# Splitting streamed weights one transfer at a time instead of one tile at a time

## The chip, the core and the metric

The kernel runs on one core of a Trainium2 chip. The metric is the device time of one execution in microseconds (us). The core has a matrix engine (TensorE, PE in the profile, its weight loads PEld), a vector engine (VectorE, DVE), a scalar engine (ScalarE, ACT), GpSimd (POOL) and SyncE (SP), which issues the DMA transfers here.

## The reference, cut to what matters

The reference is a stack of six layers on 256 tokens of width 2048, in float32: an RWKV7 mixer, a dilated attention, a pooling mixer, an RWKV7 mixer again, a layer of attention beside an RG-LRU, and an mLSTM layer, with a final norm. Every layer has the form below; the projections with their large weights are most of the work.

```python
for i in range(DEPTH):
    h = _rms_norm(x, norm_w[i])
...
    x = x + y
...
r, k, v, g = [(h + xx * mu[j]) @ w_in[j] for j in range(4)]   # RWKV7, layers 0 and 3
...
return y @ w_out, v_first
```

## The kernel before

Every projection is token-major: `proj` (L238) computes 256 tokens by 512 output columns at a time, in two PSUM tiles `qps`, and runs over the 2048 rows of the weight matrix. Activations stand, and weights are streamed from HBM. To reach float32 accuracy each operand is the sum of a high half (rounded to fp32r) and a low half (the rest), and a product is three matmuls: high activation with high weight, high with low, low with high (L258 to L261).

`weights` (L222) brings one transfer of 512 KB, that is two tiles of 128 rows by 512 columns, into a raw buffer `wr` (pool of 3) by a DMA on the SP queue (L224). Each of the two tiles is then split: ScalarE copies it into a high tile `wh` (L219), and VectorE subtracts that from the raw tile into a low tile `wl` (L220). `wh` and `wl` come from pools of 5 tiles each. In most of the RWKV7 layers every third transfer has its low tiles made on GpSimd instead (`lo_share` = 3). A tile then feeds six matmuls: two token halves by three products. One raw buffer serves two tiles, so it comes free when the second subtraction is done, and a `wh` or `wl` tile comes free when the last of its matmuls is done.

The order on each engine is written by a planner when the program is built: it traces the program in order, simulates a time line, and puts instructions that are ready into each engine's queue. Work beside the stream (attention heads, RWKV7 blocks, conversions of activations) is traced by generators that go on as the stream's pieces are traced (`pump`, `spawn`); the RWKV7 blocks are traced at a higher priority. At run time each engine goes through its queue in that order.

In an RWKV7 layer the first projections follow the mixing of `h` with its shifted difference (L496, on VectorE), then come eight blocks of heads with many small instructions, then the output projection, which adds to the residual (L398). The PSUM pool of `qps` has 2 tiles in the RWKV7 layers and 4 elsewhere. The split of whole activations uses the same helper `split` (L218) on wider tiles, for example `dh` and `dl` of 128 x 1024 in the pooling layer.

Of the kernel before, what the change touches and what calls it, by code (L numbers as in the profile page):

```python
# [12 lines left out]
FR = mybir.dt.float32r  # L13
# [14 lines left out]
# feature-major vectors: name -> rows of the source array (row-major, width), per 128-wide tile  # L28
# [45 lines left out]
def make_tables():  # L74
    """masks of the dilated attention and of the mLSTM, tables of the axial rope"""
    p, t = np.arange(128)[:, None], np.arange(128)[None]
    masks = []
    for dil in (1, 4, 16):
        row = []
        for tt, ss in ((0, 0), (1, 0), (1, 1)):  # L80
            d = (p + 128 * tt) - (t + 128 * ss)
            row.append(np.where((d >= 0) & (d <= 128 * dil) & (d % dil == 0), 0.0, -1e30))
        masks.append(np.concatenate(row, 1))
    f = np.where(p <= t, 0.0, 1e30)
    b = np.where(p >= t, 0.0, 1e30)
    odd = np.concatenate([f, 0 * f, 0 * f, b], 1)
    tok = np.arange(256)
    inv = (10000.0 ** (-np.arange(0, 64, 2) / 64)).astype(np.float32)
    ang = np.concatenate([(tok // 64).astype(np.float32)[:, None] * inv, (tok % 64).astype(np.float32)[:, None] * inv], 1)
    ax = np.stack([np.cos(ang.astype(np.float64)), np.sin(ang.astype(np.float64))], 1).reshape(2, 128, 128)  # L90
    ax = ax.transpose(1, 0, 2).reshape(128, 256)
    f32 = lambda z: np.ascontiguousarray(z, np.float32)
    return {"t_mask": f32(np.stack(masks)), "t_odd": f32(odd), "t_axial": f32(ax)}
# [5 lines left out]
# pools of the whole kernel, with their slots  # L99
KEPT = {"wr": 3, "wh": 5, "wl": 5, "ah": 4, "al": 4, "q4": 8, "z": 4, "ssq": 2, "jk": 1, "rs_v": 2, "rstd": 2, "hrstd": 2,  # L100
# [4 lines left out]
class State:  # L105
    """what a layer starts from: chunks of the normed input"""
# [9 lines left out]
class Builder:  # L116
# [20 lines left out]
    @contextmanager  # L137
    def layer(self):
        """scope of the pools that one layer uses"""
        with ExitStack() as st:  # L140
            self.lctx, self.lpools = st, {}
            yield
            self.lctx, self.lpools = None, None

    # ---------------------------------------------------------------- interleaving
    # Work beside the weight stream is traced by generators. They yield the time, in us of the tensor engine, that
    # what they wait for takes; the stream lets the due ones go on after each of its pieces.
# [37 lines left out]
    # ---------------------------------------------------------------- tiles  # L185
# [31 lines left out]
    # ---------------------------------------------------------------- splits  # L217
# [4 lines left out]
    def weights(self, src, shape):  # L222
        raw = self.t("wr", shape, F32, 3)
        self.nc.sync.dma_start(raw, src)  # L224
        self.wcount += 1
        eng = self.nc.gpsimd if self.lo_share and self.wcount % self.lo_share == 0 else None
        hi, lo = [], []
        for k in range(2):
            hi.append(self.t("wh", [128, shape[2]], FR, 5))
            lo.append(self.t("wl", [128, shape[2]], FR, 5))  # L230
            self.split(hi[k], lo[k], raw[:, k], eng)
        return hi, lo
# [4 lines left out]
    # ---------------------------------------------------------------- products  # L237
    def proj(self, w, col0, n, acts, consume, chunks=None, after=None):  # L238
        """token-major out[t, col0:col0+n] = act^T @ w; acts: (hi, lo) tiles [128, 4, 256], filled in by tasks;
        after[c]: generator to start when chunk c is used."""  # L240
        nc = self.nc
        chunks = list(range(len(acts))) if chunks is None else list(chunks)
        pts = [self.p("ps") for _ in range(2)]
        for c in chunks:
            self.drain(lambda: acts[c] is not None)
            ah, al = acts[c]
            for j in range(2):
                r0 = c * 512 + j * 256
                wh, wl = self.weights(w[r0:r0 + 256, col0:col0 + n].rearrange("(k p) n -> p k n", p=128), [128, 2, n])
                for k in range(2):  # L250
                    kk = j * 2 + k
                    st = c == chunks[0] and kk == 0
                    sp = c == chunks[-1] and kk == 3
                    for t in range(2):
                        o = pts[t][:, :n]
                        sl = slice(t * 128, t * 128 + 128)
                        nn = n
                        for u, v, x in ((ah, wh, 0), (ah, wl, 1), (al, wh, 2)):  # L258
                            for c1 in range(0, n, nn):
                                cs = slice(c1, c1 + nn)  # L260
                                nc.tensor.matmul(o[:, cs], u[:, kk, sl], v[k][:, cs], start=st and x == 0 and c1 == 0, stop=sp and x == 2, skip_group_check=True)  # L261
                    if not sp:
                        self.pump(1.29)
            if after and c in after:
                self.spawn(after[c])
        consume(pts)
        self.pump(1.29)

    def to_fm(self, src, nft, consume):
        """src token-major [128, 2, nft*128]; consume(pair index, psum [128, 2, 256]) per two feature tiles."""  # L270
# [11 lines left out]
    def acts_from(self, src, box, c, scale=None):  # L282
        """(hi, lo) chunk box[c] from a token-major [128, 2, 512]; scale(ft): per-feature column."""
# [15 lines left out]
    # ---------------------------------------------------------------- small maths  # L299
    def rsqrt(self, v, n, pre="rq"):  # L300
        """1/sqrt(v) of a small [128, n] tile (v > 0), to float32 accuracy."""
# [35 lines left out]
    def bcast(self, ap1d, tag, n, bufs=2):  # L337
        """a row of DRAM on all partitions"""
# [4 lines left out]
    # ---------------------------------------------------------------- residual, and the start of the next layer  # L343
# [93 lines left out]
    # ---------------------------------------------------------------- RWKV7  # L437
# [31 lines left out]
    def opened(self, st, u, after):  # L469
        """half a chunk of h, and its difference to the step before; its first instruction behind `after`"""  # L470
# [214 lines left out]
    def rwkv_block(self, ia, b):  # L685
        """heads 4b .. 4b+3, features 256b .. 256b+255"""
# [28 lines left out]
        # ---- normalised k, negated (token-major)  # L715
# [11 lines left out]
        # ---- decay  # L727
# [12 lines left out]
        # ---- v, with the residual of the first layer's v  # L740
# [34 lines left out]
        # ---- feature-major operands, [rt|at] / [ks|bs] for even chunks, swapped for odd ones; the other way round  # L775
        # for heads 2 and 3, so that products of 64 rows take turns on the two halves of the tensor engine's rows
# [49 lines left out]
        # ---- bonus  # L826
# [14 lines left out]
        # ---- per-chunk products  # L841
# [16 lines left out]
        # ---- inverse of the unit triangular 16 x 16 blocks by columns  # L858
# [36 lines left out]
        # ---- v above (or below) the place of the solution, and its product with the strictly lower part  # L895
# [20 lines left out]
        # ---- token-major [ks; bs] for the state  # L916
# [10 lines left out]
        # ---- doubled to 32 x 32 and 64 x 64; Y: transpose of X (whose 32 x 32 blocks off the  # L927
        # diagonal are still zero), R: of X M
# [26 lines left out]
        # the last step has one block of 32 x 32 in each of 64 x 64  # L955
# [23 lines left out]
        # ---- chunks in turn  # L979
# [58 lines left out]
        # ---- group norm, bonus  # L1038
# [28 lines left out]
    # ---------------------------------------------------------------- shared by the other layers  # L1067
# [4 lines left out]
    def silu_part(self, pts, hr, dst):  # L1072
        """dst = p (1 + tanh(hr p)); silu(rstd p) = hr dst"""
# [5 lines left out]
    def log1p_exp(self, e, shape, tag):  # L1079
        """log(1 + e) for e in [0, 1], by 2 atanh(e / (2 + e))"""  # L1080
# [23 lines left out]
    def qk_fm(self, e, nh, gain, rope, dst, box, key):  # L1104
        """rms norm over each head, gain, rope, and the transposes into dst [128, nh, 256]"""
# [18 lines left out]
    # ---------------------------------------------------------------- dilated attention  # L1124
# [29 lines left out]
    def dilated(self):  # L1154
# [68 lines left out]
        def combine(O, ml, flags):  # L1223
            # weights over the dilations; ml[:, 0] holds minus the maxima
# [81 lines left out]
    # ---------------------------------------------------------------- pool mixer  # L1306
# [73 lines left out]
    # ---------------------------------------------------------------- attention and RG-LRU  # L1380
    def even(self):
# [25 lines left out]
        # per-feature constants of the LRU  # L1407
# [193 lines left out]
    # ---------------------------------------------------------------- mLSTM  # L1601
    def odd(self):
# [13 lines left out]
        # ---- gates: g = i - b, M = max(0, cummax g), b = cumsum log sigmoid(f), per direction  # L1616
# [72 lines left out]
        def heads(u, v2, qT, kT, vt):  # L1689
# [4 lines left out]
            for a in range(2):  # L1694
# [10 lines left out]
                # blocks: forward s0 (t0 t1), backward s1 (t0 t1), backward s0 t0, forward s1 t1  # L1705
# [15 lines left out]
                for t in range(2):  # L1721
                    for d in range(2):
                        # the column of ones behind v gives the denominator
# [145 lines left out]
```

## Time and profile before

| | |
|---|---|
| median of three executions | 3269.81 us (3268.89 to 3271.18) |
| profiled execution, first to last instruction | 3273.9 us |
| its own time outside that span | not shown |
| PE busy | 3044.3 us, 93% of the span |
| DVE busy | 2383.0 us, 73% |
| ACT busy | 1789.0 us, 55% |
| POOL busy | 704.3 us, 22% |
| moved by DMA | 577.27 MB, mean 176 GB/s |

Busy times are those of one profiled execution. A matmul's end is modelled, and matmuls overlap, so 93% is not the share of time in which the engine does as much as it can. The layers follow one another at about these times: RWKV7 from 0 to 800 us, dilated attention and pooling from 800 to 1620, RWKV7 from 1620 to 2430, attention with RG-LRU to 2700, mLSTM to the end.

### The profile page before, as it was taken

To read this page: it belongs to the slowest core of one execution; us is meant where nothing else is said; L and a number is where in the kernel's file an instruction comes from. 1 tells how busy PE (TensorE), PEld (TensorE's weight loads), DVE (VectorE), ACT (ScalarE), POOL (GpSimd) and SP (SyncE) were. 2 spreads that over 40 slices of the span, in tenths; PEclk is the share of its full clock that TensorE was granted. 3 is DMA by queue.
4 is the path that set the end of the run, shared out by engine and by line. 5 is a ranking of instruction groups with operands and counts; after the bars stand their busy time and mean duration, and the time that the engine had idled before them with its cause. 6 is when DMAs were issued, how large, how long until landed. Compare 5 with 4: busy or idle time off the path is not lost.

```text
span 3273.9 us, 49521 instructions
## 1 busy us (share of the span) xinstructions
PE 3044.3 (93%) x17128; PEld 2460.4 (75%) x17128; DVE 2383.0 (73%) x5326; ACT 1789.0 (55%) x3504; POOL 704.3 (22%) x555
## 2 busy tenths in 40 slices
PE   5889989998999999999978899889989999999998
PEld 4667767776888888888756777667777788888886
DVE  7788978865667666676596888888567776666765
ACT  4566555544555555655555555544456655554554
POOL 4433433430101100020063224433311110000001
PEclk9999989999999999999988999989999999999999
DMA  5655543366565556666656644533575556666665
GB/s 180 204 187 162 169 147 116 128 196 199 176 179 178 170 174 213 200 212 190 209 163 212 198 144 152 170 112 104 192 225 160 159 180 206 181 197 171 187 185 167
DMA packets 327018, 577.27 MB, mean 176 GB/s; under 512 B 33856, under 2 KB 60776, under 8 KB 326768
## 3 DMA queue, kind: packets, MB, share of 16 engines
q1 hardware_dynamic: 326768, 574.12, 56.4%
q8 instruction: 134, 2.20, 0.3%
q14 instruction: 116, 0.95, 0.1%
HBM read 527.88 MB, written 46.15 MB: 175 GB/s over the span
## 4 chain that ended last, share of the span: by engine, by line
PE 60%; DVE 12%; DMA 5%; ACT 3%; issue 2%; POOL 1%; SPq 0%; ACTq 0%; DVEq 0%; POOLq 0%
PE qps L261 53%; DVE wl L220 3%; PE qtp L276 2%; ACT wh L219 1%; DMA wr<-a_w_out 1%; DMA wr<-a_w_in 1%; DVE e L496 1%; DMA lw<-a_a2x 1%; PE qgm L1727 1%; PE qtp L849 0%; DVE Xc L888 0%; DVE Xc L886 0%; DVE al L220 0%; DVE mb L883 0%; DMA v<-st 0%
## 5 line engine op out<-in xcount | busy, mean ns | idle before, releaser
L220 DVE TENSOR_TENSOR wl<-wr,wh 128x512 fp32r<-128x512 f32 x1580 | 1163.7, 746 | 674.1 <-ACT wh L219 660.7
L219 ACT CAST wh<-wr 128x512 fp32r<-128x512 f32 x1728 | 1055.2, 620 | 991.2 <-PE qps L261 494.9
L261 PE MATMUL qps<-wl,ah 128*128 128x512 f32 x3424 | 1387.4, 405 | 40.5 <-DVE wl L220 40.1
L261 PE MATMUL qps<-wh,al 128*128 128x512 f32 x3424 | 1371.1, 401 | 2.0 <-DVE al L220 2.0
L261 PE MATMUL qps<-wh,ah 128*128 128x512 f32 x3424 | 1270.1, 407 | 63.3 <-DVE st L398 14.5
L261 PEld LDWEIGHTS qps<-wh,ah 128*128 128x128 f32 x3424 | 658.6, 193 | 209.8 <-ACT wh L219 20.8
L261 PEld LDWEIGHTS qps<-wl,ah 128*128 128x128 f32 x3424 | 661.9, 193 | 189.2 <-DVE wl L220 55.2
L261 PEld LDWEIGHTS qps<-wh,al 128*128 128x128 f32 x3424 | 660.7, 193 | 142.0 <-DVE al L220 4.4
L220 POOL TENSOR_TENSOR wl<-wr,wh 128x512 fp32r<-128x512 f32 x148 | 201.1, 1366 | 371.0 <-ACT wh L219 326.5
L1114 POOL TENSOR_TENSOR q<-q,gain 128x1024 f32<-128x1024 f32 (+1 forms) x15 | 35.0, 2334 | 432.4 <-ACT sq L1108 432.4
L276 PE MATMUL qtp<-cst,q 128*128 128x128 f32 x388 | 61.1, 287 | 18.4 <-DMA cst<-consts 6.7
L867 ACT COPY Md<-GM 32x128 f32<-32x128 f32 x128 | 54.8, 428 | 39.7 <-DVE GM L852 38.6
L849 PE MATMUL qtp<-q,q 64*128 64x128 f32 x512 | 69.5, 300 | 6.6 <-DVE GM L852 4.7
L496 DVE SCALAR_TENSOR_TENSOR e<-q,vec,q 128x256 f32<-128x256 f32 x96 | 72.4, 801 | 0.0
L276 PEld LDWEIGHTS qtp<-cst,q 128*128 128x128 f32 x388 | 48.2, 146 | 31.2 <-issue 15.6
L883 DVE TENSOR_TENSOR mb<-mb,Xc 128x120 f32<-128x120 f32 (+14 forms) x240 | 70.2, 292 | 0.3
L219 ACT CAST ah<-st 128x512 fp32r<-128x512 f32 x64 | 38.3, 616 | 58.1 <-DMA st<-mix 57.4
L849 PEld LDWEIGHTS qtp<-q,q 64*128 64x128 f32 x512 | 56.2, 197 | 17.7 <-DVE GM L852 6.8
L220 DVE TENSOR_TENSOR al<-st,ah 128x512 fp32r<-128x512 f32 x64 | 51.9, 818 | 19.1 <-ACT ah L219 19.0
L481 POOL TENSOR_TENSOR q<-q 128x510 f32<-128x510 f32 x12 | 15.7, 1307 | 223.1 <-ACT ah L219 219.6
L498 POOL TENSOR_TENSOR e<-e,q 128x512 f32<-128x512 f32 x32 | 55.3, 1747 | 27.8 <-ACT e L494 23.9
L886 DVE TENSOR_TENSOR Xc<-Xc,mb 128x8 f32<-128x8 f32 x240 | 58.8, 245 | 0.8
(404 smaller groups left out, 3421.2 us busy)
## 6 DMA issues: line engine op xcount, KB each, us to landing
wr<-a_w_in SPq DMA_DIRECT2D x256, 512.0 KB
wr<-b_w_in SPq DMA_DIRECT2D x160, 512.0 KB
wr<-odd_w_in SPq DMA_DIRECT2D x128, 512.0 KB
wr<-even_w_in SPq DMA_DIRECT2D x72, 512.0 KB
wr<-a_w_out SPq DMA_DIRECT2D x64, 512.0 KB
wr<-c_w_in SPq DMA_DIRECT2D x64, 512.0 KB
st<-mix SPq DMA_DIRECT2D x64, 256.0 KB
wr<-c_w_out SPq DMA_DIRECT2D x32, 512.0 KB
```

The costliest lines, as they stand in the source:

```text
L219: self.nc.scalar.copy(hi, src)
L220: (eng or self.nc.vector).tensor_tensor(lo, src, hi.bitcast(F32), OP.subtract)
L261: nc.tensor.matmul(o[:, cs], u[:, kk, sl], v[k][:, cs], start=st and x == 0 and c1 == 0, stop=sp and x == 2, skip_group_check=True)
L276: nc.tensor.transpose(q[:, f, t * 128:t * 128 + 128], src[:, t, (fp * 2 + f) * 128:(fp * 2 + f) * 128 + 128], self.ident)
L496: ins = nc.vector.scalar_tensor_tensor(m[:, f], st.xx[c][:, ft], mu, st.h[c][:, ft], OP.mult, OP.add)
L498: ins = nc.gpsimd.tensor_tensor(m, m, st.h[c][:, a * 2:a * 2 + 2], OP.add)
L849: nc.tensor.matmul(qs[hp][:, c], BK[rs, f, c], AR[rs, f, c], start=True, stop=True)
L867: nc.scalar.copy(Md[rs, :, us].rearrange("p c u -> p u c"), GM2[rs, us, (1 - i // 2) ^ f, rs])
L883: nc.vector.tensor_tensor(mb[:, 0:n], mb[:, 0:n], Xc[:, r:r + 1].to_broadcast([128, n, 8]), OP.mult)
L886: nc.vector.tensor_tensor(Xc[:, r + 1], Xc[:, r + 1], mb[:, 0], OP.add)
L1114: nc.gpsimd.tensor_tensor(e3, e3, gain.unsqueeze(1).to_broadcast([128, 2 * nh, 128]), OP.mult)
L1727: nc.tensor.matmul(qn, Dm[:, blk], vt[:, s, a], start=(i == 0), stop=(i == len(tm) - 1))
```

## The change

A transfer's two tiles are split by one copy and one subtraction over 128 x 2 x 512 elements. The pools `wh` and `wl` hold four buffers of such a pair in place of five single tiles, which is eight tiles' room instead of five in each. `proj` receives views of the two tiles of a pair, and its matmuls are as they were. The reserved scratch for dynamic DMA descriptors at the start of SBUF is set to 1024 bytes per partition instead of its default. Comments and docstrings also go, which moves later line numbers by three.

```diff
-KEPT = {"wr": 3, "wh": 5, "wl": 5, "ah": 4, "al": 4, "q4": 8, "z": 4, "ssq": 2, "jk": 1, "rs_v": 2, "rstd": 2, "hrstd": 2,
+KEPT = {"wr": 3, "wh": 4, "wl": 4, "ah": 4, "al": 4, "q4": 8, "z": 4, "ssq": 2, "jk": 1, "rs_v": 2, "rstd": 2, "hrstd": 2,
...
         eng = self.nc.gpsimd if self.lo_share and self.wcount % self.lo_share == 0 else None
-        hi, lo = [], []
-        for k in range(2):
-            hi.append(self.t("wh", [128, shape[2]], FR, 5))
-            lo.append(self.t("wl", [128, shape[2]], FR, 5))
-            self.split(hi[k], lo[k], raw[:, k], eng)
-        return hi, lo
+        hi, lo = self.t("wh", shape, FR, 4), self.t("wl", shape, FR, 4)
+        self.split(hi, lo, raw, eng)
+        return [hi[:, k] for k in range(2)], [lo[:, k] for k in range(2)]
...
-    nc = bacc.Bacc("TRN2", target_bir_lowering=False, num_devices=1)
+    nc = bacc.Bacc("TRN2", target_bir_lowering=False, num_devices=1, dynamic_dma_scratch_size=1024)
```

## Rows read from the trace of the kernel before

**Rows 1.** The page: busy time by engine, and TensorE's granted clock in 40 slices.

```profile
PE 3044.3 (93%) x17128; PEld 2460.4 (75%) x17128; DVE 2383.0 (73%) x5326; ACT 1789.0 (55%) x3504; POOL 704.3 (22%) x555
...
PEclk9999989999999999999988999989999999999999
```

**Rows 2.** Windows by stage: length, busy us (instructions) of PE, PEld, DVE, ACT, POOL, clock, DMA share, GB/s.

```profile
0.00:200.00 200.00, 148.62 (x635) 114.19 (x636) 152.47 (x239) 111.02 (x223) 82.58 (x68) 0.92 0.59 193
200.00:700.00 500.00, 459.17 (x3722) 361.23 (x3720) 415.22 (x1304) 275.96 (x609) 185.63 (x153) 0.95 0.47 150
...
800.00:1620.00 820.00, 818.41 (x3838) 680.79 (x3838) 552.36 (x942) 460.15 (x837) 75.94 (x51) 1.00 0.62 189
1620.00:1850.00 230.00, 190.06 (x881) 151.78 (x880) 178.85 (x305) 130.22 (x257) 87.27 (x64) 0.90 0.60 190
1850.00:2330.00 480.00, 436.99 (x3525) 341.67 (x3524) 396.33 (x1259) 252.29 (x562) 167.92 (x142) 0.93 0.45 142
```

**Rows 3.** The chain that ended last, whole span: shares by line, pieces (start, us, what).

```profile
by line: PE qps L261 52.8%; DVE wl L220 2.9%; issue 2.1%; PE qtp L276 1.6%; ACT wh L219 1.1%; DMA wr<-a_w_out 1.0%; DMA wr<-a_w_in 1.0%; DVE e L496 0.8%; DMA lw<-a_a2x 0.8%; PE qgm L1727 0.6%; PE qtp L849 0.5%; DVE Xc L888 0.5%; DVE Xc L886
...
1388.31 27.25 PE qps L261 x120
...
2366.70 5.29 DMA wr<-a_w_out
```

**Rows 4.** The same chain, from 1625 to 1850 us, then from 1850 to 2330 us.

```profile
by line: DVE e L496 12.2%; DMA wr<-a_w_in 12.0%; DVE wl L220 10.3%; PE qps L261 9.5%; issue 9.0%; DMA mix<-st 4.3%; ACT wh L219 4.1%; DMA v<-st 3.7%; DVE al L220 3.0%; POOL e L498 2.6%; ACT e L494 2.5%; ACT ah L219 2.1%; DVE q L477 2.0%; DM
...
by line: PE qps L261 25.8%; DVE wl L220 6.4%; DMA lw<-a_a2x 5.5%; issue 4.8%; PE qtp L849 2.6%; DVE Xc L886 2.6%; DVE mb L883 2.1%; DMA st<-mix 1.8%; DVE Xc L888 1.8%; DMA vt<-v 1.8%; PE qtp L731 1.8%; DVE e L755 1.7%; ACT wh L219 1.7%; DVE
981 pieces in order of time: start us, us, what
```

**Rows 5.** Lines 219 and 220: duration ns min/median/max, first and last start us.

```profile
L219 ACT CAST wh<-wr x1728: 600/621/671, 13.8 to 3251.8; 128x512 fp32r<-128x512 f32 x192
L219 ACT CAST dh<-q x4: 1048/1051/1054, 1369.7 to 1457.9; 128x1024 fp32r<-128x1024 f32 x4
...
L220 DVE TENSOR_TENSOR wl<-wr,wh x1580: 617/691/2893, 14.6 to 3252.5; 128x512 fp32r<-128x512 f32 x198
L220 POOL TENSOR_TENSOR wl<-wr,wh x148: 1262/1290/2243, 209.4 to 2390.2; 128x512 fp32r<-128x512 f32 x148
L220 DVE TENSOR_TENSOR dl<-q,dh x4: 1225/1225/1227, 1370.7 to 1459.0; 128x1024 fp32r<-128x1024 f32 x4
```

**Rows 6.** Timeline of ACT and DVE: pairs of splits back to back (start, us).

```profile
2372.07 1.14 ACT L219 CAST wh<-wr 128x512 fp32r<-128x512 f32 x2 [1.72 <-DMA wr<-a_w_out]
...
2406.35 1.28 DVE L220 TENSOR_TENSOR wl<-wr,wh 128x512 fp32r<-128x512 f32 x2
```

**Rows 7.** Waits, whole span: who waited for whom, us in total, times, longest.

```profile
ACT wh L219 <- PE qps L261: 494.9, 569, 9.5
...
PEld qps L261 <- DVE wl L220: 55.6, 35, 5.5
PEld qps L261 <- ACT wh L219: 21.0, 9, 4.3
PE qps L261 <- DVE wl L220: 40.1, 25, 5.1
PE qps L261 <- ACT wh L219: 14.2, 6, 3.9
```

**Rows 8.** Waits of weight loads from 0 to 545 us, then from 1620 to 2430 us.

```profile
PEld qps L261 <- DVE wl L220: 28.3, 19, 3.7
...
PEld qps L261 <- DVE wl L220: 18.5, 9, 5.5
```

**Rows 9.** Timeline of PE behind a stall (start, us, [idle before and releaser]).

```profile
2381.10 0.76 PE L261 MATMUL qps<-wh,ah 128*128 128x512 f32 x1 [3.96 <-DVE st L398]
2381.66 0.63 PE L261 MATMUL qps<-wl,ah 128*128 128x512 f32 x1
2382.09 0.63 PE L261 MATMUL qps<-wh,al 128*128 128x512 f32 x1
```

## The prediction, made before the changed kernel ran

> **What bounds the kernel now.** The table by engine [rows 1] says that TensorE is busy for 93% of the span and VectorE for 73%, but these are means over unlike stages, so the windows come next. From 800 to 1620 us TensorE is busy for 818.41 of 820 us at a granted clock of 1.00, with VectorE at 552 and ScalarE at 460 [rows 2]. There the chain of waits runs through unbroken stretches of the stream: 120 matmuls in 27.25 us [rows 3], 0.227 us each. A tile's six matmuls take 1.36 us and a transfer's twelve 2.72. Both splits of a transfer cost less than that on either engine (below), so in such a stage a cheaper split buys nothing. The last layer runs the same way.
>
> The two RWKV7 layers are different. In their openings (0 to 200 us, 1620 to 1850) TensorE is busy for 149 of 200 and 190 of 230 us, its clock is 0.92 and 0.90, and VectorE is busy for 152 and 179 us [rows 2]. In the blocks (200 to 700, 1850 to 2330) VectorE is at 83% and TensorE at 91 to 92%, again below full clock. The chain in the second opening consists of VectorE's mixing (12.2%), weight transfers (12.0%) and low halves (10.3%); in the second layer's blocks TensorE's stream leads it (25.8%), then low halves (6.4%) and many small pieces [rows 4]. If the change matters, it matters in these layers, some 1,600 us of the span.
>
> The last view is the waits. ScalarE waited for TensorE to free a `wh` tile for 494.9 us in 569 waits [rows 7]: most of the time the buffers are full and the splits are ahead. TensorE in turn waited on splits for little: its weight loads 55.6 us for low tiles (35 waits) and 21.0 for high ones (9); its matmuls 40.1 and 14.2, mostly the same stalls seen a second time [rows 7]. Of the 55.6, the first 545 us hold 28.3 and the second RWKV7 layer 18.5 [rows 8].
>
> **The change, part by part.** *Price of a split.* By the rows for lines 219 and 220, two narrow copies take 2 x 0.621 = 1.242 us and one of 128 x 1024 takes 1.051; two narrow subtractions take 2 x 0.691 = 1.382 and a wide one 1.225 [rows 5]. By duration a transfer saves 0.191 us on ScalarE and 0.157 on VectorE; over 1728/2 = 864 copies and 1580/2 = 790 subtractions that is 165 and 124 us of work. Durations overlap, however, when instructions follow each other: two copies take 1.14 us together and two subtractions 1.28 [rows 6], so the second adds 0.52 and 0.59. With the same overlap of 0.10 a wide one adds 0.95 and 1.125, and a transfer saves 0.09 and 0.06. GpSimd's 148 low tiles become 74 pairs; no row has its wide subtraction, which I bound by 2 x 1.290 = 2.58 us and by that times 1.225/1.382, 2.29. GpSimd is hardly used apart from this in those stages, so it gets nothing in the sum.
>
> What counts is the share on the path. The chain has 2.9% of 3273.9 us = 95 us of low tiles and 1.1% = 36 of high ones [rows 3]. Its first piece that the profile gives is at about 540 us, so I let the second layer stand for the missing part: 10.3% and 4.1% of 225 us for the opening, 6.4% and 1.7% of 320 us for the blocks, 44 and 15 us [rows 4]. On 139 and 51 us the saving by durations (11.4% and 15.4%) is 16 + 8 = 24 us; by spacing (0.06 of 1.18, 0.09 of 1.04, so 5% and 9%) it is 7 + 5 = 12. VectorE in these stages is near 80% busy, where instructions mostly queue, so I take 12. Everywhere else the saving is covered by TensorE's 2.72 us per transfer; without that cover it would be worth the 0.15 us per transfer.
>
> *The first tile comes later.* With narrow splits the first tile of a landed transfer is ready after 0.621 + 0.691 = 1.31 us and the second after 0.621 + 2 x 0.691 = 2.00. With wide ones both are ready after 1.051 + 1.225 = 2.28: 0.97 us later for the first, 0.28 for the second [rows 5]. This costs only where TensorE truly waits on a split, at most 35 + 9 = 44 times [rows 7]. Bounds: 0, if deeper buffers cover all of them, and 44 x 0.97 = 43 us, if each is for a first tile. In the openings VectorE works through the halves one after another with mixing between, so the second tile is what holds TensorE back next; I take 35 x 0.28 = 10 us.
>
> *More buffers.* Five tiles hold 5 x 1.36 = 6.8 us of TensorE's work, eight hold 10.9. With three raw buffers the stream can be about seven transfers ahead instead of five. That could remove at most the 55.6 + 21.0 = 77 us of waits [rows 7], and with each the slow matmuls behind it: after a stall of 3.96 us TensorE went on with 0.43 us between matmuls instead of 0.227 [rows 9], the half level of its clock (1.2 GHz instead of 2.4) for a short while. At least it removes nothing. But 47 of 56 us lie in the RWKV7 layers [rows 8], mostly with VectorE's own work late, which more buffers only let it do a little earlier; I take a fifth of the 77, 15 us.
>
> *Longer instructions in the queues.* An urgent small instruction that becomes ready during a subtraction waits half of 1.225 us instead of half of 0.691 on the average, 0.27 more. From 200 to 700 us VectorE is in splits for about a quarter of the time, so a handover costs some 0.07 us more. Of the 981 chain pieces between 1850 and 2330 [rows 4] perhaps a quarter are such handovers: 17 us in a layer, 34 in two. The lower bound is nothing, because the planner knows the durations and arranges the queue by them. I take 8.
>
> *A raw buffer is held longer.* It is free 0.28 us later per turn, against a transfer that took 5.29 us on the chain [rows 3]. The chain's two large groups of weight transfers, 2.0% or 65 us, are about 12 turns, so 3 us at most; the deeper store pays for it, and I take 0. The queue on SP keeps its order of transfers. The smaller scratch touches no instruction that the trace shows: all transfers of the program's data are issued on SP.
>
> Sum: -12 + 10 - 15 + 8 = -9 us. The profiled execution's span would go from 3273.9 to about 3265. It is 4 us above the median of the runs; the time around the span isn't shown, so I carry the difference over: 3269.8 - 9 = 3261 us.
>
> **The rivals.** *A: the saving stays hidden.* The buffers are full most of the time (494.9 us of ScalarE's waits, [rows 7]), two thirds of the span are TensorE's, and the terms above are small and of both signs. The time is 3270 us. Against it: 139 us of low tiles on the chain. That the larger store never fills, because three raw buffers can't feed it, ends here as well.
>
> *B: the deeper store is what counts.* If three more tiles remove nearly all stalls of the matmuls on splits (54 us) and the other terms are as above with no late first tile, the sum is -54 - 12 + 8 = -58: 3212 us. For it speaks that a stall also costs clock; against it, that so few stalls lie in the blocks, where a store could have been filled beforehand.
>
> *C: slower, by the first tile.* In the two openings TensorE waits for what was just split: 19 + 9 = 28 waits [rows 8]. If the buffers are empty there, each is 0.97 us longer, 27 us, and the deeper store gives nothing: 27 - 12 + 8 = +23, so 3293 us. It decides from the point where more than four or five waits are for a first tile and the store removes none (4 x 0.97 against 12 - 8).
> The Trainium skill, Perfetto Trace Analysis, section Optimizing Scalar/DVE Operations, says that larger operations help where the engine is saturated, and that where ScalarE or VectorE are not saturated but cause bubbles elsewhere, breaking instructions up lets work finish sooner. VectorE at 73% overall and 76 to 78% in the openings is not saturated [rows 2], so by that rule the change goes the wrong way there, and the time would be that of C.
>
> **How the numbers follow.** The forecast, a small gain, has 0.37; A 0.27; B 0.10; C 0.26. Three executions lie within 2.3 us; 0.2%, or 6.5 us, is about what a measurement tells from no change. Faster by more is the forecast and B, 0.47; within it A, 0.27; slower C, 0.26. The planner will write every queue anew, and a chain of a thousand pieces may shift by ten or twenty us for that alone. The range goes from 3225 (the saving by durations, 24, and half of the 54 us of matmul stalls, with the 8 against them: -43, or 3227) to 3292 (next to C), and leaves out about two in ten. The forecast's own range is 3240 to 3263.
>
> **What would show it.** The wide copy at about 1.05 us x864 and the wide subtraction at about 1.23 x790 show the prices. From 800 to 1620 us the same work should take the same 820 us. ScalarE's waits for TensorE should be half as many. If the store is right, the weight loads' waits on `wl` fall below 40 us, and the clock in the openings rises above 0.92 and 0.90; if C is, they rise to 80 or more in the same places. I am wrong if the second RWKV7 layer's blocks change by more than 20 us either way without a change in those waits: then the new order of the queues did it. I am wrong as well if the stages that are TensorE's alone get longer, which would mean that a pair's later release starves the stream.

## The result, and the profile after

The changed kernel takes 3302.98 us (median of four executions, 3295.3 to 3304.65) against 3270.35 for the kernel before, a ratio of 1.0095 (95% interval 1.0075 to 1.0114): 31 us slower by the ratio. The forecast was 3261 with a range up to 3292.

The page of the changed kernel, busy time by engine and the granted clock, beside [rows 1]:

```profile
span 3299.6 us, 47015 instructions
PE 3051.0 (92%) x17128; PEld 2473.7 (75%) x17128; DVE 2296.0 (70%) x4536; ACT 1656.2 (50%) x2640; POOL 712.8 (22%) x481
...
PEclk9989999999999999999989989988989999999999
```

VectorE has lost 87 us of work and ScalarE 133, and the kernel is slower. The prices of the splits were as read from [rows 5]; lines 219 and 220 after, with duration in ns (min/median/max) and first and last start:

```profile
L219 ACT CAST wh<-wr x864: 1027/1053/1083, 21.2 to 3273.5; 128x1024 fp32r<-128x1024 f32 x173
...
L220 DVE TENSOR_TENSOR wl<-wr,wh x790: 1149/1225/3406, 22.3 to 3274.6; 128x1024 fp32r<-128x1024 f32 x198
L220 POOL TENSOR_TENSOR wl<-wr,wh x74: 2342/2394/3247, 206.2 to 2400.9; 128x1024 fp32r<-128x1024 f32 x74
```

The store worked as well. Waits of the changed kernel on splits, beside [rows 7]:

```profile
ACT wh L219 <- PE qps L258: 673.7, 439, 6.2
...
PEld qps L258 <- DVE wl L220: 15.4, 12, 4.3
...
PEld qps L258 <- ACT wh L219: 7.2, 3, 6.0
```

Weight loads waited 15.4 us for low tiles instead of 55.6, and 7.2 for high ones instead of 21.0. Where TensorE waited for the stream, it hardly does now. So the loss is elsewhere. The first transfers of the layers' weights mark the stages (durations in ns of the issue, first and last start in us):

```profile
L224 SPq DMA_DIRECT2D wr<-b_w_in x160: 367/368/384, 785.8 to 1280.6; - x160
...
L224 SPq DMA_DIRECT2D wr<-even_w_in x72: 367/368/1899, 2435.1 to 2687.6; - x72
...
L224 SPq DMA_DIRECT2D wr<-odd_w_out x32: 367/368/368, 3179.6 to 3268.7; - x32
```

Before, these began at 775.3, 2414.0 and 3157.9 us. By these marks the first RWKV7 layer has cost 10 us, and the second brings the delay to 21. With a deeper store a transfer can be issued further ahead of its use, so such marks may be early. The last addition to the residual of each layer (L398 before, L395 after) gives the end of the layer: 791.0 and 801.7 us for the first RWKV7 layer, 2429.6 and 2451.0 for the second, 2777.3 and 2802.4 for attention with RG-LRU (which ends at 2777 us and not at 2700), 3258.8 and 3284.4 for the last. The two RWKV7 layers add 11 and 14 us, the layer after the second adds 4, and the last adds nothing. The last step of the RWKV7 blocks (16 blocks; before it ran from 345.9 to 2384.5 us) moves more:

```profile
L1053 POOL TENSOR_TENSOR yt<-yt,vt x16: 1257/1294/2306, 362.9 to 2423.5; 128x512 f32<-128x512 f32 x16
```

The first block ends 17 us later, the last 39, so the layer ends with half of its last block's delay. Windows of the changed kernel, columns as in [rows 2]:

```profile
200.00:700.00 500.00, 454.37 (x3655) 359.80 (x3654) 404.28 (x1231) 257.77 (x504) 166.77 (x117) 0.93 0.46 144
1850.00:2330.00 480.00, 433.63 (x3411) 339.24 (x3410) 389.03 (x1208) 237.09 (x462) 159.81 (x112) 0.90 0.43 137
800.00:1620.00 820.00, 815.92 (x3835) 679.41 (x3834) 521.97 (x692) 418.16 (x574) 85.81 (x51) 1.00 0.63 190
```

From 800 to 1620 us nothing changes for TensorE (3835 matmuls against 3838 at a clock of 1.00). Beside the blocks it starts fewer matmuls in the same time (3411 against 3525 from 1850 to 2330) at a lower clock (0.90 against 0.93, 0.93 against 0.95 in the first layer). About half of the missing matmuls come from the later start of the stretch: from 1865 to 2345 us there are 3472, again at 0.90. What grew there are handovers within the blocks and the conversions of activations; waits of the changed kernel:

```profile
ACT Md L864 <- DVE GM L849: 55.5, 19, 5.6
...
ACT yt L1030 <- PE qgy L1026: 35.3, 22, 4.7
ACT uv L1006 <- PE qgy L1002: 34.2, 17, 10.3
...
DVE al L220 <- ACT ah L219: 48.0, 26, 6.6
```

Before they were 38.6, 26.5, 27.2 and 24.9 us: 117 together, now 173. The growth is not the loss itself: four narrow pairs (below), as fast as the kernel before, have 46.7, 58.0, 28.8 and 40.0 us in the same groups, 174 together.

### The profile page after: what moved, and what is told of

It is laid out like the page before. It is cut to its first block, busy times and chain, and to the rows that moved or that the text cites. A ratio compares the mean times of both kernels' runs of the same rounds, so it can differ in the third digit from the quotient of the medians.

```text
span 3299.6 us, 47015 instructions
## 1 busy us (share of the span) xinstructions
PE 3051.0 (92%) x17128; PEld 2473.7 (75%) x17128; DVE 2296.0 (70%) x4536; ACT 1656.2 (50%) x2640; POOL 712.8 (22%) x481
## 3 DMA queue, kind: packets, MB, share of 16 engines
q1 hardware_dynamic: 326768, 574.12, 56.4%
## 4 chain that ended last, share of the span: by engine, by line
PE 56%; DVE 11%; DMA 7%; issue 3%; ACT 3%; POOL 2%; SPq 0%; ACTq 0%; DVEq 0%; POOLq 0%
PE qps L258 49%; DVE wl L220 3%; PE qtp L273 2%; DMA wr<-a_w_in 1%; DMA wr<-a_w_out 1%; ACT wh L219 1%; DVE e L493 1%; DMA lw<-a_a2x 1%; PE qgm L1724 1%; DMA v<-st 1%; DMA mix<-st 1%; DVE al L220 0%; PE qtp L846 0%; POOL wl L220 0%; DMA st<-mix 0%
## 5 line engine op out<-in xcount | busy, mean ns | idle before, releaser
L220 DVE TENSOR_TENSOR wl<-wr,wh 128x1024 fp32r<-128x1024 f32 x790 | 1027.9, 1304 | 695.2 <-ACT wh L219 693.1
L258 PE MATMUL qps<-wh,ah 128*128 128x512 f32 x3424 | 1378.3, 405 | 58.3 <-ACT st L604 16.6
L258 PE MATMUL qps<-wh,al 128*128 128x512 f32 x3424 | 1376.5, 404 | 10.8 <-DVE al L220 10.7
L219 ACT CAST wh<-wr 128x1024 fp32r<-128x1024 f32 x864 | 905.8, 1050 | 915.0 <-PE qps L258 673.7
L258 PEld LDWEIGHTS qps<-wl,ah 128*128 128x128 f32 x3424 | 661.9, 193 | 152.4 <-DVE wl L220 15.4
L220 POOL TENSOR_TENSOR wl<-wr,wh 128x1024 fp32r<-128x1024 f32 x74 | 184.3, 2491 | 362.1 <-ACT wh L219 356.5
L493 DVE SCALAR_TENSOR_TENSOR e<-q,vec,q 128x256 f32<-128x256 f32 x96 | 80.0, 880 | 0.0
L585 POOL TENSOR_TENSOR GM<-e,GM 128x512 fp32r<-128x512 f32 x32 | 66.1, 2088 | 10.0 <-ACT GM L584 10.0
```

What stands on the lines that cost most here:

```text
L219: self.nc.scalar.copy(hi, src)
L220: (eng or self.nc.vector).tensor_tensor(lo, src, hi.bitcast(F32), OP.subtract)
L493: ins = nc.vector.scalar_tensor_tensor(m[:, f], st.xx[c][:, ft], mu, st.h[c][:, ft], OP.mult, OP.add)
L585: nc.gpsimd.tensor_tensor(hl[:, 1, s], m, hl[:, 0, s].bitcast(F32), OP.subtract)
```

## The experiments

Two things are in the change, the width of a split and the depth of the store. The theory after the result: one of them, or both, delays the RWKV7 blocks. The rival: the planner's new order of the queues did it, and either alone means nothing. All kernels below use the small descriptor scratch, except the kernel before with another planner's price. With the small scratch alone the program differs from the one before in addresses only; the instructions stand in the same order on every engine. No run times it alone. "Narrow" is a split per tile, "wide" a split per transfer. Each run's ratio is to the kernel before, timed beside it on the same chip, with its 95% interval.

**Width and depth, crossed.** Narrow splits into pairs, in place of the change's one line; three pairs is 3 for 4 in the pools:

```diff
-        self.split(hi, lo, raw, eng)
+        for k in range(2):
+            self.split(hi[:, k], lo[:, k], raw[:, k], eng)
```

> Four buffers of pairs as in the change, but each tile split by its own copy and subtraction. If the length of an instruction is the cause, about 3270 us. If the store's depth or its release by pairs is, about 3300 us. If only the order is, anywhere between 3255 and 3305.

> Wide splits with three buffers of pairs instead of four, six tiles' room against five before. If the length is the cause, it stays slow, 3295 to 3310 us, a little more than the change because less is in store. If the depth is the cause, it is near before, 3270 to 3280 us.

> Three buffers of pairs and narrow splits: neither the length nor the depth of the change, but its release by pairs. If length or depth is the cause, about 3270 us, at most 10 us more for the coarser release. If the release by pairs is, or the new order alone, it can be 3290 us or more.

| three raw buffers | narrow | wide |
|---|---|---|
| three pairs | 3249 us, 0.9937 (0.9915 to 0.9959) | 3275 us, 1.0014 (0.9999 to 1.0028) |
| four pairs | 3271 us, 0.9998 (0.9985 to 1.0011) | 3303 us, 1.0095 (1.0075 to 1.0114) |

Neither theory had it whole. The first step of the change, from five single tiles to four pairs with narrow splits, costs nothing (0.9998); the second, going wide, costs all of it. Going wide costs 26 us with three pairs and 32 with four; a fourth pair costs 22 narrow and 28 wide. The two add up. Three narrow pairs are faster than the kernel before, which was not expected: six tiles' room, in units of two.

**Single tiles.** The kernel before with eight and with six tiles in each pool:

```diff
-KEPT = {"wr": 3, "wh": 5, "wl": 5, ...
+KEPT = {"wr": 3, "wh": 8, "wl": 8, ...
```

> Eight single tiles in each pool, split one tile at a time: the room of the change without its wide instructions. If the length of the wide splits is what delays the RWKV7 blocks, this is no slower than before: 3270 us or less. If the deeper store is (more splits standing ahead of the blocks' instructions in the queues), it is as slow as the change, about 3300 us. If the new order of the queues alone is, anything from 3255 to 3305 is possible.

> Six single tiles, the room of three pairs, released and refilled one at a time. If the depth sets the time, it lies between five tiles (3270 us) and eight (3285), about 3275. If the release by pairs is what makes three pairs fast, it does not come near 3249; if the room of six is, it does.

Eight: 3285 us, 1.0041 (1.0030 to 1.0051). Six: 3269 us, 1.0002 (0.9986 to 1.0019). So depth without any wide split costs 15 us, half of what the depth theory said. Room for six is not what makes three pairs fast: with the same room, 3249 as pairs and 3269 as singles; with room for eight, 3271 and 3285. Releasing and refilling by pairs came with a gain of some 14 to 20 us with narrow splits, not much more than another order alone can move (below).

**Less in store.**

> Two pairs and narrow splits: four tiles. If less in store is better all the way, below 3249 us. If the store is needed to carry TensorE over the splits, it runs dry: 3265 us or more, with more waits on low tiles than the 55.6 us of before.

3306 us, 1.0098 (1.0077 to 1.0118). Less is not better all the way. The store runs dry, as these rows show (waits of weight loads with two narrow pairs, against 55.6 and 21.0 in [rows 7]):

```profile
PEld qps L259 <- DVE wl L220: 115.6, 98, 7.4
PEld qps L259 <- ACT wh L219: 23.9, 22, 2.8
```

**Which instruction.** Four pairs, with the copy wide and the subtractions per tile, and the other way round:

```diff
-        self.split(hi, lo, raw, eng)
+        self.nc.scalar.copy(hi, raw)
+        for k in range(2):
+            (eng or self.nc.vector).tensor_tensor(lo[:, k], raw[:, k], hi[:, k].bitcast(F32), OP.subtract)
```

> Four buffers of pairs, the copy wide and the subtraction narrow. Four pairs with narrow splits took 3271 us and with wide ones 3303. If the long instruction on VectorE is the cause, this is near 3271; if it is the one on ScalarE (and the subtractions that wait for it), near 3303; if each adds its part, about 3287.

> The counterpart: the copy narrow and the subtraction wide. Near 3303 us if VectorE's long instruction is the cause, near 3271 if ScalarE's is, about 3287 if each adds its part.

Wide copy: 3295 us, 1.0090 (1.0064 to 1.0116). Wide subtraction: 3286 us, 1.0057 (1.0040 to 1.0074). The wide copy alone does nearly all of the harm of both (narrow 3271, both wide 3303), the wide subtraction alone about half or more. So it isn't the length of one engine's instruction.

**Where.** Wide splits except in the RWKV7 layers, with four pairs and with three:

```diff
-        self.split(hi, lo, raw, eng)
+        if self.banks["ps"] == 2:
+            for k in range(2):
+                self.split(hi[:, k], lo[:, k], raw[:, k], eng)
+        else:
+            self.split(hi, lo, raw, eng)
```

> The change, but with narrow splits in the two RWKV7 layers alone. If the wide splits do harm beside the blocks only, this gives the time of narrow splits everywhere, 3271 us, within 10. If they do harm in the other layers too, it stays above 3285.

> Three buffers of pairs, narrow splits in the RWKV7 layers and wide ones in the others: what the experiments so far point to. If length hurts only beside the blocks and depth too, this is as fast as three pairs with narrow splits everywhere, 3249 us, within 8.

Four pairs: 3268 us, 1.0004 (0.9993 to 1.0015), against 1.0095 with wide splits everywhere. Three pairs: 3246 us, 0.9934 (0.9919 to 0.9949), against 0.9937 with narrow ones everywhere. With three raw buffers width does its harm in the RWKV7 layers alone; elsewhere it neither costs nor pays, though it takes work off both engines. The switch covers a whole layer, its opening and its output projection too, so the runs don't say that it is beside the blocks.

**Shorter still.** In the RWKV7 layers a tile in two halves of 256 columns, four pairs:

> Four buffers of pairs; in the RWKV7 layers each tile is split by two copies and two subtractions of 256 columns, elsewhere by one of each of 512. If the blocks suffer from the length of one instruction, halving it again gives less than the 3271 us of narrow splits, by up to 15. If the work on VectorE and ScalarE is what counts, the extra instructions make it slower, 3280 or more.

3272 us, 1.0006 (0.9995 to 1.0018), the same as whole tiles. Halving the length once more buys nothing. That speaks against length in the queues as such, but not firmly: the extra instructions keep VectorE busy for 12 us more than with narrow splits and ScalarE for 57 (2387.2 and 1788.2 us against 2375.3 and 1731.6), which may hide a gain.

**Is it the order alone?** The planner's price of a piece changed by a hundredth, in the kernel before, in the change, and with three narrow pairs:

```diff
-                        self.pump(1.29)
+                        self.pump(1.28)
```

> The kernel before, with the planner's price of one piece of the stream at 1.28 us instead of 1.29: the same work and the same buffers, in slightly different order. If a new order alone moves the time by tens of us, this is 15 us or more away from 3270, and what was seen between depths and lengths of splits may be chance. If it is within 8 us, those differences stand.

> The change with the planner's price of a piece at 1.28 us instead of 1.29: the same splits in another order. If the wide splits with the deep store are the cause, 3295 to 3310 us again, as 3303. If the order drawn by the planner was unlucky, it can come back to 3280 or less.

> Three pairs and narrow splits with the planner's price at 1.28 us. If the gain of that version is the depth's, it stays near 3249 us, within 10. If it was luck of the order, it goes to 3265 or more.

Before: 3261 us, 0.9985 (0.9972 to 0.9998). The change: 3311 us, 1.0133 (1.0118 to 1.0148). Three narrow pairs: 3238 us, 0.9914 (0.9897 to 0.9930). A new order of the same work moves the time by 5 to 11 us, and the three versions keep their places. The rival falls as the whole cause: the change was slower in both orders drawn, by 33 and by 50 us. Two orders of a version are a small sample all the same.

**Depth beside the blocks, not tested.** Four narrow pairs, one of each pool meant to be taken at the start of an RWKV7 layer and given back at its end:

```diff
         self.banks = BANKS[True]
+        held = [self.t("wh", [128, 2, 512], FR, 4), self.t("wl", [128, 2, 512], FR, 4)]
+        for x in held:
+            nc.gpsimd.memset(x[:, 0, 0:2].bitcast(F32), 0.0)
...
+        back = self.t("rs_v", [128, 2], F32, 2)
+        for x in held:
+            nc.gpsimd.tensor_copy(back, x[:, 0, 0:2].bitcast(F32))
```

> Four pairs and narrow splits as in the run of 3271 us, but one pair of each pool is held unused through each RWKV7 layer, so that three are there beside the blocks and four in the other layers. If the depth costs beside the blocks alone, about 3249 us, as with three pairs everywhere; if it costs elsewhere too, or if what helps three pairs is something else, about 3270.

3283 us, 1.0035 (1.0020 to 1.0050): a miss on both sides, but the edit did not do what it was meant to. The planner put the copies that give the pair back right behind the writes that take it, as the first and last starts of both show (one in each RWKV7 layer):

```profile
L488 POOL MEMSET wh<- x2: 100/100/100, 0.7 to 1625.0; 128x2 f32 x2
...
L678 POOL COPY rs_v<-wh x2: 188/188/188, 7.7 to 1625.2; 128x2 f32<-128x2 f32 x2
```

The pair was held for about 7 us in the first layer and under 1 in the second, and from then on four pairs stood beside the blocks. The run says nothing on depth. It is one more order of four narrow pairs, with eight tiny instructions on GpSimd, 12 us from the run of 3271.

**Raw buffers.** The change with two raw buffers; then three pairs with four raw buffers, narrow and wide:

```diff
-KEPT = {"wr": 3, "wh": 4, "wl": 4, ...
+KEPT = {"wr": 4, "wh": 3, "wl": 3, ...
```

> The change with two raw buffers instead of three: six transfers ahead instead of seven, but the same four split pairs. If the harm of the deep store is that of split pairs standing ahead, still 3300 us or more. If it is that of more transfers in flight, beside which the blocks' own loads come late, it falls to 3290 or less.

> Three pairs, narrow splits and four raw buffers instead of three. Two raw buffers starved the stream, so if three are still a little short, this is faster than the 3249 us of the same with three; if three are enough it is 3249, and if transfers further ahead disturb the blocks, 3260 or more.

> The same with wide splits, which took 3275 us with three raw buffers. A wide split holds its raw buffer longer. If that is the harm, a fourth raw buffer removes it and the two runs come within 8 us of each other. If the length of the instructions is, 20 us or more stay between them.

Two raw buffers: 3501 us, 1.0693 (1.0674 to 1.0712). The loss is spread over all layers, since ScalarE now waits for transfers everywhere (waits of that run):

```profile
ACT wh L219 <- DMA wr<-a_w_in: 218.0, 116, 7.4
ACT wh L219 <- DMA wr<-b_w_in: 204.0, 113, 4.9
ACT wh L219 <- DMA wr<-odd_w_in: 182.1, 98, 4.1
```

Against the change, of which this is a variant, 3501 us is 6.0% more. That is a new bottleneck, and it tells nothing about depth. It shows that two raw buffers are too few, not how near three are to that. Four raw buffers, narrow: 3262 us, 0.9977 (0.9964 to 0.9990). Wide: 3241 us, 0.9908 (0.9889 to 0.9928). With a fourth raw buffer wide splits are no longer slower than narrow ones, but 21 us faster; they were 26 us slower with three. ScalarE's waits for transfers in three wide kernels, first the change (four pairs, three raw), then three pairs with three raw, then three pairs with four raw:

```profile
ACT wh L219 <- DMA wr<-a_w_in: 76.2, 34, 7.1
...
ACT wh L219 <- DMA wr<-a_w_out: 46.2, 21, 5.8
```

```profile
ACT wh L219 <- DMA wr<-a_w_in: 69.6, 29, 7.1
...
ACT wh L219 <- DMA wr<-a_w_out: 32.5, 17, 4.5
```

```profile
ACT wh L219 <- DMA wr<-a_w_in: 17.8, 6, 7.3
...
ACT wh L219 <- DMA wr<-a_w_out: 8.6, 3, 3.4
```

For the RWKV7 weights they sum to 122, 102 and 26 us; the times are 3303, 3275 and 3241. The narrow kernels do not follow this series. The same waits for four pairs with three raw buffers, then three pairs with three, then three pairs with four:

```profile
ACT wh L219 <- DMA wr<-a_w_in: 83.0, 38, 7.0
...
ACT wh L219 <- DMA wr<-a_w_out: 35.2, 18, 6.5
```

```profile
ACT wh L219 <- DMA wr<-a_w_in: 62.9, 29, 6.7
...
ACT wh L219 <- DMA wr<-a_w_out: 26.4, 12, 4.4
```

```profile
ACT wh L219 <- DMA wr<-a_w_in: 32.9, 13, 6.8
...
ACT wh L219 <- DMA wr<-a_w_out: 10.8, 5, 3.6
```

Here they sum to 118, 89 and 44 us, and the times are 3271, 3249 and 3262. Going wide with three raw buffers adds 4 us of these waits with four pairs and 13 with three, against 32 and 26 us of time; and narrow splits lost 46 us of waits with the fourth buffer and became 13 us slower. So these waits do not carry the cost of width. Blocks in the last wide kernel run at a clock of 0.95 and 0.93, as in the kernel before (windows as in [rows 2]):

```profile
200.00:700.00 500.00, 457.06 (x3716) 359.70 (x3714) 407.95 (x1239) 258.94 (x507) 178.21 (x121) 0.95 0.46 150
1850.00:2330.00 480.00, 429.44 (x3487) 337.84 (x3487) 382.41 (x1153) 237.36 (x466) 169.34 (x112) 0.93 0.42 139
```

So with three pairs the harm of width goes with the number of raw buffers, and length in the queues can't be its cause by itself: the instructions are as long with four. Four pairs, as in the change, were not run with a fourth raw buffer.

## Why the prediction was wrong

*Prices.* Right: 1.053 and 1.225 us, and GpSimd's pair at 2.394 between the bounds of 2.29 and 2.58. TensorE's own stages kept their time. One reading was wrong: GpSimd is not hardly used apart from the low tiles. In the four windows of [rows 2] it is busy for 523 us, and its 148 low tiles take about 191 [rows 5]. The saving was taken as 12 us on the path; wide splits outside the RWKV7 layers gained nothing that could be measured, and inside them the work saved was outweighed.

*A raw buffer is held longer.* This step failed: "3 us at most", taken as 0. With it the terms of width came to 6 us (-12 + 10 + 8 + 0). With three raw buffers, as in the change, width cost 32 us at four pairs and 26 at three; with four raw buffers and three pairs it gained 21. The row used, the share of weight transfers on the chain, doesn't show how short the ring of three is. What is shown is that the cost of width goes with the number of raw buffers: a swing of 47 us, where another order of the same work moved times by 5 to 12. The reserve is that three of these four kernels ran in one order only. That the longer hold is the reason is not shown. By the prediction's own working a raw buffer is held for 2.00 us with narrow splits and 2.28 with wide ones. With the copy alone wide it would be 1.051 + 2 x 0.691 = 2.43, and with the subtraction alone 2 x 0.621 + 1.225 = 2.47 (an estimate from [rows 5]). These two should then have been slower than the change; they were about 8 and 17 us faster. ScalarE's waits for transfers don't show it either. By which way width delays the RWKV7 layers stays open.

*More buffers.* This step was wrong in size, too: 15 us of gain forecast, none measured, as four narrow pairs take the time of the kernel before (0.9998). Yet they removed 59 of the 77 us of waits (10.8 and 6.6 us are left), and the whole change removed 54. Three comparisons of like kinds give 22, 28 and 15 us of loss for the greater depth, so more buffers may cost, where the prediction's lower bound was nothing; the gain that came with pairs hides it in the change. Waits that stand in a list are not time on the path. Nor does the end of the last block set the end of the layer: with four narrow pairs that block ended 8 us later than before (2392.7 against 2384.5) and the layer 11 us earlier (2418.9 against 2429.6), in a profiled execution 6 us below that kernel's median. Why the depth costs stays open.

*The first tile comes later* (10 us) did not show in the change: against narrow splits with the same four pairs, waits of weight loads on low tiles went from 10.8 to 15.4 us, 5 of the 32. With three pairs and three raw buffers they went from 34.9 to 59.5, as much as the 26 us of time, so there this step may be at work; it wasn't tested apart. With the fourth raw buffer they went from 53.1 to 49.4.

*Longer instructions* (8 us, at most 34) named the RWKV7 layers, where the loss is, but halving the splits again changed nothing, and with a fourth raw buffer long splits did no harm. The blocks' handovers did grow, by 56 us over four groups, but by as much with four narrow pairs, which cost no time.

*The rivals.* C had the sign and nearly the time, 3293, by luck: its mechanism did not happen. It wanted waits on low tiles of 80 us or more in the openings, and there were 15.4 in the whole span. The sentence of the Trainium skill that stands with it (Perfetto Trace Analysis, section Optimizing Scalar/DVE Operations: breaking up instructions where the engine isn't saturated) gave the right direction with three raw buffers, by 26 and 32 us, and the wrong one with four, by 21; breaking them up further did nothing (1.0006). The last paragraph of the prediction named what was seen: in the second layer the time from the end of the first block to that of the last grew from 393 to 431 us, without more waits on splits. It put that down to the new order; the reordered kernels moved by 5 to 11 us as a whole, and the change stayed slower.

The fastest versions were three pairs with wide splits and four raw buffers, 0.9908, and three narrow pairs with the planner's price at 1.28, 0.9914.

## What to carry to other kernels

When a stage of the pipeline gets coarser, count the hold time of every buffer it reads as well as of those it fills, and time the coarse and the fine version with one source buffer more: here that turned 26 us of loss into 21 of gain. A run with one buffer fewer only shows that fewer is too few. A list of waits removed is no gain until the work that ends the stage is seen to start earlier. Where a planner writes the queues, draw a second order of each version before believing a difference under half a per cent, and look in the trace whether an instruction that was meant to come late did.

## What was not expected of the hardware

Two raw buffers of 512 KB instead of three cost the changed kernel 6.0%, although its DMA engines were busy for little more than half of the time with three (56.4% of the 16 engines' span). And the same program of splits, 87 and 133 us lighter on two engines that are not idle, was 31 us slower: TensorE's granted clock over the span went from 0.962 to 0.957 with the change, and stood at 0.969 in the version with wide splits and four raw buffers.
